# Mixer's last 32 tokens on a quarter of the array's columns, and a near 1/rms ahead of the exact one

## The chip, the cores and the metric

The kernel runs on one core of a Trainium2 chip. The metric is the device time of one execution in microseconds (us). TensorE (PE in the profile) multiplies, VectorE (DVE), ScalarE (ACT) and GpSimd (POOL) do the elementwise work, and SyncE (SP) issues the transfers. Each engine works its own queue in order; between engines there are semaphores.

## The reference, cut to what matters

The reference is a decoder trunk of two layers over 272 tokens (16 meta tokens and 256 others) of width 1024. Each layer is a half-step SwiGLU FFN, a mixer, and another half-step FFN, each between two RMSNorms. The first layer's mixer is a causal pooling mixer, the second layer's is differential attention. The part that the change is about is the pooling mixer and the norm behind it:

```python
def causal_multiscale_pool(h, w, b, scale):     # windows 2, 4, 8, 16 over four groups of 256 columns
    ...
    for g, win in enumerate(POOL_WINDOWS):
        lo = jnp.maximum(t + 1 - win, 0)
        cnt = (t + 1 - lo).astype(jnp.float32)
        pooled.append((csg[:, 1:, g] - csg[:, lo, g]) / cnt[None, :, None])
    diff = (jnp.stack(pooled, axis=2) - hg).astype(h.dtype)
    y = jnp.einsum('blgc,gcd->blgd', diff, w) + b
    return y.reshape(bsz, L, D) * scale
# in the trunk
    m = causal_multiscale_pool(rmsnorm(h, mix_norm_pre[i]), pool_w[j], pool_b[j], pool_scale[j])
    h = h + rmsnorm(m, mix_norm_post[i])
    f = swiglu(rmsnorm(h, ffn_norm_pre[i, 1]), ffn_w1[i, 1], ffn_w3[i, 1], ffn_w2[i, 1])
```

## The kernel before, in words

The residual h lies with the 1024 columns on partitions, as eight tiles of 128 x 272 (j = 0 to 7). The kernel has four FFN stages (ffn(0) to ffn(2) and last_ffn), the pooling mixer (`pool_mix`) between ffn(0) and ffn(1), and attention with its output projection (`attn_out`) between ffn(2) and last_ffn. Large products are made of three fp32r matmuls each: weights and activations are split into a high part (ACT, line 136: `whi`; `xhi`) and a low part (DVE, line 148: `wlo`; `xlo`), and lines 254 to 256 multiply high by high, high by low, low by high. Elsewhere matmuls are plain fp32, and the profile shows two records (two weight loads, two matmuls) for each of these.

The order of work on PE, ACT, DVE and SP is the order in which the program is written; no scheduler moves anything there.

**The mixer.** `inner(j)` (line 673) multiplies each h tile by its 128 x 256 weight `wp`, as soon as the tile has got the residual of ffn(0): line 691 makes the product `pt`, line 692 adds it to `h`, all on DVE in row pairs (1), (2, 3), (4, 5), (6, 7). Its output is token-major, for three blocks of tokens: 0 to 127, 128 to 255, and the last 128, of which only the last 32 matter (16 tokens and the 16 meta tokens, which stand last). ACT squares h (line 694, `psq`), DVE sums the squares (lines 698 to 701, `pacc`), and PE adds them over partitions (line 703, `sums`). From this comes 1/rms for each token (lines 280 and 274 to 276, `ny`), and ACT and DVE copy the inner products out of the PSUM banks scaled by it (lines 712 to 717, `zs`). `pooled(j)` (lines 725, 726, 729) then multiplies by constant band matrices (`bands`), which do the windowed mean and the subtraction.

**Behind the mixer.** ACT squares each y_j (line 445, `sq`), DVE sums the squares (line 456) and makes some of the scaled tiles `bt` (line 438: j = 0, 3, 4 in between, and j = 1, 2, 5 of `BESIDE` at the end). `post.rms` sums over partitions (lines 462 and 463), and line 280 makes 1/rms, `ny`. The first three tiles of ffn(1)'s input are made ahead from it: `rt` = b * ny (line 311), `xhi` = a + rt (line 313), where `a` (line 424) and `b` (line 429) were made earlier by ACT. `first_blocks` (line 514) then runs PE over these three (`go`), and goes on with the tiles that need the refined 1/rms (`refine`, lines 494, 326, 497, 328; then `tile`, lines 343 to 358), of which the first here is tile 3.

The three other such places already have a near 1/rms: the last squares are rounded to fp32r (line 470, `sqr`) and summed by single-pass matmuls (line 480), PE starts with the high parts, and the exact sum follows later (line 488).

**The output projection.** In `attn_out` ACT squares and scales each of the first five outputs (lines 445 and 436) between the splits of weights (line 136); `lows` (line 1043) waits for the squares of line 470.

Of the kernel before, what the change touches and what calls it, by code (L numbers as in the profile page):

```python
# [41 lines left out]
OUT_TABLE = 2  # L42

# [8 lines left out]
LATE = 2  # L52

POOL_H = ((0, 1), (1, 2), (2, 4), (4, 6), (6, 8))
POOL_SQ = ((0, 2), (2, 4), (4, 6), (6, 8))
# [10 lines left out]
BESIDE = (1, 2, 5)  # L66
REFILL = (0, 0, 0, 0, 0, 0, 0, 2)
# [111 lines left out]
def trunk(ctx, tc, ht, w13a, w13b, w2t, w2n, wqkva, wqkv, wo, wp, lamv, mask, band, gpost, out):  # L179
# [214 lines left out]
    class Post:  # L394


        def __init__(self, n, gains, next_gain, ahead):
            self.n, self.gains, self.next, self.ahead, self.acc = n, gains, next_gain, ahead, None
            self.r = None
            self.near, self.nears = False, []  # L400
            self.ab = []
            self.bt = [None] * NK
            self.sq = [None] * NK
# [64 lines left out]
        def near_square(self, j, y):  # L468
            sq = tmp.tile([P, L], F32R, tag="rsq", name="sqr", bufs=3)
            nc.scalar.activation(out=sq[:, :self.n], in_=y, func=AF.Square)  # L470
            self.nears.append((j, sq))

        def rms_near(self, bank, eps=False):
# [9 lines left out]
            w.refill(1, held=0)  # L483
# [19 lines left out]
    def first_blocks(res, us, spans, sums, refill, order):  # L503
# [153 lines left out]
    def pool_mix(old, ps, post):  # L657
# [17 lines left out]

        with tc.tile_pool(name="poolw", bufs=1, reuse_waits="tile") as pw:
            sq = pw.tile([P, NK, L], F32, name="psq")
            zs = [pw.tile([P, D], F32, name=f"zs{ti}", tag=f"zs{ti}") for ti in range(3)]
            ys = []

# [8 lines left out]
            for lo, hi in POOL_H[1:]:  # L689
                t = pw.tile([P, 3, L], F32, tag="pt", name="pt", bufs=2)[:, :hi - lo]  # L690
                nc.vector.tensor_tensor(t, btall[:, lo:hi], old.r.unsqueeze(1).to_broadcast([P, hi - lo, L]), ALU.mult)
                nc.vector.tensor_tensor(hall[:, lo:hi], hall[:, lo:hi], t, ALU.add)
# [5 lines left out]
            nc.vector.tensor_tensor(acc, sq[:, 0:2], sq[:, 2:4], ALU.add)  # L698
            nc.vector.tensor_tensor(acc, acc, sq[:, 4:6], ALU.add)
            nc.vector.tensor_tensor(acc, acc, sq[:, 6:8], ALU.add)  # L700
            nc.vector.tensor_tensor(acc[:, 0], acc[:, 0], acc[:, 1], ALU.add)
            for ti, (t0, t1) in enumerate(tok):
                nc.tensor.matmul(sums[:, ti:ti + 1], lhsT=acc[:, 0, t0:t1], rhs=ones[:, 0:1], start=True, stop=True)
# [6 lines left out]
            def normed(q):  # L710
                at = slice(q * 512, (q + 1) * 512)
                nc.scalar.mul(out=zs[0][:, at], in_=z[q][0], mul=r2[:, 0:1])
                nc.vector.tensor_scalar(zs[1][:, at], z[q][1], r2[:, 1:2], None, ALU.mult)
                if q:
                    nc.vector.tensor_scalar(zs[2][:, at], z[q][2], r2[:, 2:3], None, ALU.mult)
                else:
                    nc.scalar.mul(out=zs[2][:, at], in_=z[q][2], mul=r2[:, 2:3])

            def pooled(j):
# [5 lines left out]
                nc.tensor.matmul(y[:, P:SEQ], lhsT=zs[1][:, c], rhs=bands[:, g, 0:P], start=True, stop=True)  # L725
# [542 lines left out]
```

## Time and profile before

| what | before |
|---|---|
| median of 3 runs | 956.22 us (955.8 to 956.35) |
| the profiled execution, its own time | 956.16 us |
| its span, first to last instruction | 954.4 us |
| PE / DVE / ACT / POOL busy | 942.7 / 610.2 / 502.9 / 15.3 us |
| mean granted TensorE clock | 0.999 |

The span is the time between the first and the last instruction that the profiler recorded; the 1.76 us that the execution's own time has more lie around it. The busy times are unions of records. PE's records overlap and their ends are modelled, so a busy PE is not a PE at its best; where PE waits is read from the starts of its records and from the chain of waits.

### The profile page before, as it was taken

What the parts mean: (1) busy time and instruction counts of PE and PEld (TensorE: products, weight loads), DVE (VectorE), ACT (ScalarE), POOL (GpSimd) and SP (SyncE); (2) the same over time, 40 slices, a digit from 0 to 9 for tenths busy, and PEclk for the clock granted to TensorE, in tenths of its full rate; (3) what the DMA queues carried; (4) which work ended last, traced back from release to release, by engine and by line L of the source; (5) the groups of instructions that cost most, each with busy time, mean ns of one, the idle gap of its engine ahead of it and who ended that gap; (6) DMA issues with size and microseconds to landing.
All of it is one profiled execution on the core that took longest, in us unless ns stands there. A gap on an engine that the chain in (4) does not pass through costs nothing.

```text
span 954.4 us, 17970 instructions
## 1 busy us (share of the span) xinstructions
PE 942.7 (99%) x7241; PEld 918.6 (96%) x7241; DVE 610.2 (64%) x1054; ACT 502.9 (53%) x865; POOL 15.3 (2%) x22
## 2 busy tenths in 40 slices
PE   9999999999999999999999999999999999999997
PEld 9999999998999999999999999999998999999996
DVE  7955554458975555448855554478877898555553
ACT  7744444435654445545744455446767766444432
POOL 0000000210000000000000000000001000000000
PEclk9999999999999999999999999999999999999999
DMA  9765557630375556551755566522533628555521
GB/s 333 242 203 178 168 157 217 223 113 1 133 260 171 171 160 200 175 191 45 255 187 177 166 174 191 179 98 90 177 103 119 221 100 298 183 193 180 179 84 44
DMA packets 48322, 160.77 MB, mean 168 GB/s; under 512 B 5360, under 2 KB 8944, under 8 KB 48240
## 3 DMA queue, kind: packets, MB, share of 16 engines
q1 hardware_dynamic: 47952, 159.31, 51.3%
q8 instruction: 56, 0.92, 0.4%
q10 hardware_dynamic: 288, 0.33, 0.1%
q14 instruction: 26, 0.21, 0.1%
HBM read 158.57 MB, written 1.05 MB: 167 GB/s over the span
## 4 chain that ended last, share of the span: by engine, by line
PE 94%; DVE 3%; ACT 2%; issue 1%; DVEq 0%; POOL 0%; ACTq 0%; POOLq 0%
PE bank L256 26%; PE bank L255 26%; PE bank L254 26%; PE bank L514 8%; ACT whi L136 1%; PE bank L626 1%; PE bank L638 1%; PE bank L627 1%; PE bank L268 0%; ACT sc L827 0%; PE bank L804 0%; PE bank L795 0%; PE bank L794 0%; DVE h L343 0%; PE bank L1043 0%
## 5 line engine op out<-in xcount | busy, mean ns | idle before, releaser
L148 DVE TENSOR_TENSOR wlo<-raw,whi 128x1024 fp32r<-128x1024 f32 (+1 forms) x296 | 353.3, 1197 | 58.7 <-PE bank L255 28.5
L254 PE MATMUL bank<-xhi,whi 128*128 128x272 f32 (+1 forms) x1360 | 390.8, 287 | 0.0
L256 PE MATMUL bank<-xlo,whi 128*128 128x272 f32 (+1 forms) x1360 | 390.2, 287 | 0.0
L255 PE MATMUL bank<-xhi,wlo 128*128 128x272 f32 (+1 forms) x1360 | 389.0, 286 | 0.2 <-DVE wlo L148 0.2
L136 ACT CAST whi<-raw 128x1024 fp32r<-128x1024 f32 (+1 forms) x296 | 299.8, 1029 | 50.8 <-PE bank L256 45.9
L255 PEld LDWEIGHTS bank<-xhi,wlo 128*128 128x128 f32 x1360 | 256.0, 188 | 1.0 <-DVE wlo L148 0.4
L254 PEld LDWEIGHTS bank<-xhi,whi 128*128 128x128 f32 x1360 | 256.0, 188 | 1.0 <-issue 0.4
L256 PEld LDWEIGHTS bank<-xlo,whi 128*128 128x128 f32 x1360 | 256.5, 189 | 0.0
L255 PE MATMUL bank<-ghi,wlo 128*128 128x272 f32 x484 | 140.2, 290 | 0.0
L254 PE MATMUL bank<-ghi,whi 128*128 128x272 f32 x484 | 140.1, 289 | 0.0
L256 PE MATMUL bank<-glo,whi 128*128 128x272 f32 x484 | 140.0, 289 | 0.0
L556 ACT ACTIVATE ua<-ua 128x272 f32<-128x272 f32 (+1 forms) x88 | 37.0, 429 | 143.3 <-DVE ua L551 143.3
L562 DVE TENSOR_TENSOR ua<-bank,ua 128x272 f32<-128x272 f32 (+1 forms) x88 | 37.6, 435 | 93.6 <-PE bank L256 93.6
L565 ACT CAST ghi<-ua 128x272 fp32r<-128x272 f32 (+1 forms) x88 | 36.2, 418 | 110.6 <-DVE ua L562 110.6
L551 DVE TENSOR_TENSOR ua<-bank,ny 128x272 f32<-128x272 f32 (+1 forms) x88 | 37.6, 435 | 88.8 <-PE bank L256 88.8
L254 PEld LDWEIGHTS bank<-ghi,whi 128*128 128x128 f32 x484 | 91.9, 190 | 0.0
L256 PEld LDWEIGHTS bank<-glo,whi 128*128 128x128 f32 x484 | 91.4, 189 | 0.0
L255 PEld LDWEIGHTS bank<-ghi,wlo 128*128 128x128 f32 x484 | 91.0, 188 | 0.0
L456 DVE TENSOR_TENSOR pacc<-pacc,sq 128x272 f32<-128x272 f32 (+1 forms) x34 | 14.9, 438 | 42.0 <-ACT sq L445 41.5
L514 PE MATMUL bank<-xhi,whi 128*128 128x272 f32 (+1 forms) x240 | 38.0, 295 | 1.8 <-DVE xhi L313 1.7
L571 DVE TENSOR_TENSOR glo<-ua,ghi 128x272 fp32r<-128x272 f32 (+1 forms) x88 | 37.2, 431 | 0.5 <-ACT ghi L565 0.5
L514 PE MATMUL bank<-xhi,wlo 128*128 128x272 f32 (+1 forms) x240 | 36.9, 290 | 0.0
(207 smaller groups left out, 926.5 us busy)
## 6 DMA issues: line engine op xcount, KB each, us to landing
raw<-in_w13b SPq DMA_DIRECT2D x152, 512.0 KB, 3.8
raw<-in_w2t SPq DMA_DIRECT2D x48, 448.0 KB, 3.4
raw<-in_w2t SPq DMA_DIRECT2D x24, 512.0 KB, 3.6
raw<-in_w2n SPq DMA_DIRECT2D x22, 512.0 KB, 3.3
raw<-in_w13a SPq DMA_DIRECT2D x18, 512.0 KB, 3.3
raw<-in_wqkv SPq DMA_DIRECT2D x18, 512.0 KB, 3.4
raw<-in_wo SPq DMA_DIRECT2D x8, 512.0 KB, 3.2
raw<-in_wqkva SPq DMA_DIRECT2D x6, 512.0 KB, 3.2
```

Source lines behind the costliest of these rows:

```text
L136: self.nc.scalar.copy(out=hi[:, :n], in_=self.raws[u][:, :n])
L148: self.nc.vector.tensor_tensor(lo[:, :n], raw[:, :n], hi[:, :n].bitcast(F32), ALU.subtract)
L254: nc.tensor.matmul(out_ap, lhsT=a[0], rhs=b[0], start=start, stop=False)
L255: nc.tensor.matmul(out_ap, lhsT=a[1], rhs=b[0], start=False, stop=False)
L256: nc.tensor.matmul(out_ap, lhsT=a[0], rhs=b[1], start=False, stop=stop)
L456: nc.vector.tensor_tensor(acc[:, :n], self.acc[:, :n], sq[:, :n], ALU.add)
L514: nc.tensor.matmul(us[q][:, :n], lhsT=taken[u][a][:, c * P:(c + 1) * P], rhs=x[:, :n], start=start, stop=stop)
L551: nc.vector.tensor_tensor(a[:, :self.n], u1[:, :self.n], self.r2[:, :self.n], ALU.mult)
L556: nc.scalar.activation(out=a[:, :self.n], in_=a[:, :self.n], func=AF.Silu)
L562: nc.vector.tensor_tensor(s[:, :n], u3[:, :n], s[:, :n], ALU.mult)
L565: nc.scalar.copy(out=hi, in_=s[:, :n])
L571: nc.vector.tensor_tensor(lo, s[:, :self.n], hi.bitcast(F32), ALU.subtract)
```

## The change

Five things change.

1. The inner product of the last 32 tokens gets a bank of its own, `ze`, with one group of columns on each quarter of its partitions: eight matmuls with 32 stationary columns (`inner_ends`), behind `sums`. `inner` is left with two blocks of tokens. To give the sums for that bank, POOL adds the last 32 columns of the two halves of the squares, four times side by side (`spread`).
2. 1/rms is no longer applied to the inner products but to the band matrices: the products are copied out plainly, and ACT, DVE and POOL scale the bands (`sb`). `post.old` (`a`) is made behind this.
3. POOL adds the residual to h tiles 6 and 7 (`update`), the order of `inner` becomes 0, 1, 2, 3, 6, 7, 4, 5, and the squares and their sums follow it.
4. The mixer's last two squares (j = 6, 7) are rounded to fp32r for a near 1/rms (`rms_near`). The exact squares come later, and the exact sum and the refinement are done behind the second of the three tiles that were made ahead (`exact_at = 1`).
5. In `attn_out`, the scaled tiles 2 and 3 are made by DVE instead of ACT (`OUT_VECTOR`).

```diff
+OUT_VECTOR = (2, 3)
+POOL_NEAR = 6
...
@@ Post
-            if bias is None:
+            if bias is None and vector:
+                nc.vector.tensor_scalar(o, y, g, None, ALU.mult)
+            elif bias is None:
                 nc.scalar.mul(out=o, in_=y, mul=g)
@@ first_blocks
-            if k == EXACT[res.n] and res.post.near:
+            if res.post.near and k == res.post.exact_at:
                 res.post.exact()
                 res.refine()
@@ pool_mix
-        tok = ((0, P), (P, 2 * P), (L - P, L))
+        tok = ((0, P), (P, 2 * P))
+        ze = bank()
...
+        def inner_ends():
+            for j in (0, 2, 4, 6, 1, 3, 5, 7):
+                g = slice(j // 2 * 32, j // 2 * 32 + 32)
+                nc.tensor.matmul(ze[g, 0:256], lhsT=h[j][:, L - 32:L], rhs=wps[j], start=j % 2 == 0, stop=j % 2 == 1)
...
+            def update(engine, lo, hi):
+                t = pw.tile([P, 2, L], F32, tag="pt", name="pt", bufs=3)[:, :hi - lo]
+                engine.tensor_tensor(t, btall[:, lo:hi], old.r.unsqueeze(1).to_broadcast([P, hi - lo, L]), ALU.mult)
+                engine.tensor_tensor(hall[:, lo:hi], hall[:, lo:hi], t, ALU.add)
...
-            for lo, hi in POOL_H[1:]:
-                t = pw.tile([P, 3, L], F32, tag="pt", name="pt", bufs=2)[:, :hi - lo]
-                nc.vector.tensor_tensor(t, btall[:, lo:hi], old.r.unsqueeze(1).to_broadcast([P, hi - lo, L]), ALU.mult)
-                nc.vector.tensor_tensor(hall[:, lo:hi], hall[:, lo:hi], t, ALU.add)
-            for lo, hi in POOL_SQ:
-                nc.scalar.activation(out=sq[:, lo:hi], in_=hall[:, lo:hi], func=AF.Square)
-            for j in range(NK - LATE):
+            update(nc.gpsimd, 6, 8)
+            update(nc.vector, 1, 2)
+            inner(0)
+            inner(1)
+            squares(0, 2)
+            update(nc.vector, 2, 4)
+            inner(2)
+            inner(3)
+            squares(2, 4)
+            update(nc.vector, 4, 6)
+            squares(6, 8)
+            squares(4, 6)
+            for j in (6, 7, 4, 5):
                 inner(j)
+            nc.scalar.copy(out=zs[0][:, 0:512], in_=z[0][0])
+            nc.scalar.copy(out=zs[1][:, 0:512], in_=z[0][1])
...
+            nc.gpsimd.tensor_tensor(spread, two[0], two[1], ALU.add)
+            nc.vector.tensor_tensor(total, acc[:, 0], acc[:, 1], ALU.add)
             for ti, (t0, t1) in enumerate(tok):
-                nc.tensor.matmul(sums[:, ti:ti + 1], lhsT=acc[:, 0, t0:t1], rhs=ones[:, 0:1], start=True, stop=True)
-            for j in range(NK - LATE, NK):
-                inner(j)
+                nc.tensor.matmul(sums[:, ti:ti + 1], lhsT=total[:, t0:t1], rhs=ones[:, 0:1], start=True, stop=True)
+            nc.tensor.matmul(sums[:, 2:3], lhsT=spread.rearrange("p a b -> p (a b)"), rhs=ones[:, 0:1], start=True, stop=True)
+            inner_ends()
+            nc.vector.tensor_copy(zs[1][:, 512:1024], z[1][1])
+            nc.scalar.copy(out=zs[0][:, 512:1024], in_=z[1][0])
+            r2 = rsqrt(sums, 3, True, "rc", 3)
+            for q in range(2):
+                g = slice(2 * q, 2 * q + 2)
+                nc.scalar.mul(out=sb[:, g, 0:P + NMETA], in_=bands[:, g, 0:P + NMETA], mul=r2[:, 0:1])
+                nc.vector.tensor_scalar(sb[:, g, 176:], bands[:, g, 0:P], r2[:, 1:2], None, ALU.mult)
+                nc.gpsimd.tensor_scalar(sb[:, g, P + NMETA:176], bands[:, g, P + NMETA:], r2[:, 2:3], None, ALU.mult)
+                if q == 0:
+                    nc.scalar.copy(out=zse, in_=ze[:, 0:256])
             for j in range(post.ahead):
                 post.old(j)
-            r2 = rsqrt(sums, 3, True, "rc", 3)
...
-                post.squared(j, y[:, :L], vt[:, C_PS + j:C_PS + j + 1], pbs[:, j:j + 1], add=False)
-                if j:
+                if j >= POOL_NEAR:
+                    post.near_square(j, y[:, :L], vt[:, C_PS + j:C_PS + j + 1], pbs[:, j:j + 1])
+                else:
+                    squared(j)
+                if 0 < j <= POOL_NEAR:
                     post.add(j - 1)
...
-            for j in range(1, post.ahead):
-                first(j)
+            first(1)
             for j in BESIDE:
                 scaled(j, True)
-            post.rms(lambda: s, True)
+            post.rms_near(lambda: s, True, 0)
+            for j in range(POOL_NEAR, NK):
+                squared(j)
+            for j in range(2, post.ahead):
+                first(j)
             for j in range(NK):
                 if j not in EARLY + BESIDE:
                     scaled(j)
+            post.exact_at = 1
@@ attn_out
-            post.scaled(j, ys[j][:, :n])
+            post.scaled(j, ys[j][:, :n], vector=j in OUT_VECTOR)
```

In the rows below, a name is a tile, `x6` says how many instructions of the kind follow one another, and the shape is that of the result. PE between the residual of ffn(0) and the first `pooled`, before:

```order
L268 MATMUL bank<-ones 128x128 x12
L673 MATMUL bank<-wp,h 128x256 x18
L703 MATMUL bank<-ones,pacc_2635 128x1 x3
L673 MATMUL bank<-wp,h 128x256 x6
L725 MATMUL bank<-bands,zs_2590 128x128
L726 MATMUL bank<-bands,zs_2589 128x144
L729 MATMUL bank<-bands,zs_2591 128x2x16
```

and PE at the same place after the change:

```order
L267 MATMUL bank<-ones 128x128 x12
L674 MATMUL bank<-wp,h 128x256 x16
L731 MATMUL bank<-ones,ptotal 128x1 x2
L732 MATMUL bank<-ones,spread 128x1
L680 MATMUL bank<-wp,h 32x256 x8
L754 MATMUL bank<-sb,zs_2589 128x128
L755 MATMUL bank<-sb,zs_2588 128x144
L758 MATMUL bank<-sb,zse 128x2x16
```

All sixteen inner products now stand ahead of the sums, and the eight quarter products stand where six whole ones stood.

DVE from the residual's factor `r` to the sum of the squares, before:

```order
L501 SCALAR_TENSOR_TENSOR r_2599<-nt,ny 128x272
L691 TENSOR_TENSOR pt<-bt,r_2599 128x272
L692 TENSOR_TENSOR h<-h,pt 128x272
L691 TENSOR_TENSOR pt<-bt,r_2599 128x544
L692 TENSOR_TENSOR h<-h,pt 128x544
L691 TENSOR_TENSOR pt<-bt,r_2599 128x544
L692 TENSOR_TENSOR h<-h,pt 128x544
L691 TENSOR_TENSOR pt<-bt,r_2599 128x544
L692 TENSOR_TENSOR h<-h,pt 128x544
L698 TENSOR_TENSOR pacc_2635<-psq 128x544
```

and what POOL has in all after the weights `wp` of the mixer, after the change (before, the first and the last of these rows follow one another):

```order
L650 TENSOR_SCALAR wp<-wp,h 128x256 x8
L690 TENSOR_TENSOR pt<-bt,r_2598 128x544
L691 TENSOR_TENSOR h<-h,pt 128x544
L727 TENSOR_TENSOR spread<-pacc_2634 128x128
L742 TENSOR_SCALAR sb<-bands,ny 128x2x32 x2
L421 TENSOR_SCALAR a<-h 128x256 x4
```

The last pair of DVE's rows of `pt` and `h` (lines 691 and 692, 544 elements) has moved to POOL, where it stands beside the three pairs that DVE keeps.

PE at the start of ffn(1), before:

```order
L463 MATMUL bank<-sq,ones 128x272
L514 MATMUL bank<-xhi,whi 128x272 x6
L514 MATMUL bank<-xhi,wlo 128x272 x6
L514 MATMUL bank<-xhi,whi 128x272 x6
L514 MATMUL bank<-xhi,wlo 128x272 x6
L514 MATMUL bank<-xhi,whi 128x272 x6
L514 MATMUL bank<-xhi,wlo 128x272 x6
```

and after the change:

```order
L481 MATMUL bank<-sqr,ones_r 128x272 x2
L515 MATMUL bank<-xhi,whi 128x272 x6
L515 MATMUL bank<-xhi,wlo 128x272 x6
L515 MATMUL bank<-xhi,whi 128x272 x6
L515 MATMUL bank<-xhi,wlo 128x272 x6
L489 MATMUL bank<-pacc,ones 128x272
L515 MATMUL bank<-xhi,whi 128x272 x6
L515 MATMUL bank<-xhi,wlo 128x272 x6
```

The exact sum (line 489) stands between the second and the third of the tiles made ahead, and the third is all that PE has between the exact sum and tile 3.

More of the change, by code (lines that the diff above doesn't have):

```diff
@@ L466, in rms, with near_square, rms_near @@
             self.y = rsqrt_table(self.s, n, eps, "r1")
[L468 removed]
+        def near_square(self, j, y, scale=1.0, bias=0.0):
             sq = tmp.tile([P, L], F32R, tag="rsq", name="sqr", bufs=3)
[L470 removed]
+            nc.scalar.activation(out=sq[:, :self.n], in_=y, func=AF.Square, scale=scale, bias=bias)
             self.nears.append((j, sq))
[L473 removed]
+        def rms_near(self, bank, eps=False, refill=1):
             n = self.n
@@ L1242, in _layout @@
     count = np.minimum(np.concatenate([t[NMETA:], t[:NMETA]]) + 1, win)
+    each = np.where((d >= 0) & (d < win), 1.0 / count, 0.0) - (d == 0)
     ends = np.zeros((P, 4, 2 * NMETA))
-    ends[P - NMETA:] = np.where((d >= 0) & (d < win), 1.0 / count, 0.0) - (d == 0)
+    for g in range(4):
+        ends[g * 32 + NMETA:g * 32 + 32, g] = each[:, g]
     r["band"] = c(np.concatenate([inside, ends], axis=2).astype(np.float32))
```

39 lines of the change are left out of this document (17 added, 22 removed).

## The prediction

> **What bounds the kernel now.** I read the page first: how much of the span is PE, and what the chain of waits is made of.
>
> ```profile
> PE 942.7 (99%) x7241; PEld 918.6 (96%) x7241; DVE 610.2 (64%) x1054; ACT 502.9 (53%) x865; POOL 15.3 (2%) x22
> PE 94%; DVE 3%; ACT 2%; issue 1%; DVEq 0%; POOL 0%; ACTq 0%; POOLq 0%
> ```
>
> PE bounds nearly everything; the 6% of the chain on DVE and ACT lies where the stages meet. So the second view is the chain of waits between ffn(0) and ffn(1) (start, us, engine, line):
>
> ```profile
> 209.94 0.45 DVE pt L691
> 210.42 0.44 DVE h L692
> ...
> 213.65 0.65 DVE pt L691
> 214.32 0.74 DVE h L692
> ...
> 217.88 0.83 PE bank L703 x6
> 218.70 2.70 PE bank L673 x12
> ...
> 226.94 0.58 ACT sq L445
> 227.52 0.48 ACT b L429
> 228.02 1.50 DVE bt L438 x3
> 229.52 0.36 DVE rt L311
> ...
> 230.49 0.61 PE bank L514 x3
> ```
>
> DVE's residual and sums lead to line 703 at 217.88, two inner products on PE to `pooled`, PE's eight `pooled` to the last square, and then neither PE nor `ny` but ACT's `b` and three `bt` on DVE to the first `xhi`. From the end of the last square to ffn(1) it is 230.49 - 227.52 = 2.97 us. The third view is the order of time, for what stands beside this chain:
>
> ```profile
> 209.59 8.19 PE L673 MATMUL bank<-wp,h 128*128 128x256 f32 x36
> 212.33 5.05 PEld L673 LDWEIGHTS bank<-wp,h 128*128 128x128 f32 x24 [0.23 <-issue]
> 215.65 1.33 ACT L424 ACTIVATE a<-h 128x272 f32<-128x272 f32 x3
> 219.50 0.16 DVE L276 SCALAR_TENSOR_TENSOR ny<-nt,ny 128x3 f32<-128x3 f32 x1
> 221.24 0.39 PE L725 MATMUL bank<-bands,zs 128*128 128x128 f32 x2
> 222.05 0.58 ACT L445 ACTIVATE sq<-bank,pbs,h 128x272 f32<-128x272 f32 x1 [0.51 <-PE bank L729]
> 222.53 0.57 ACT L429 ACTIVATE b<-bank,pfirst 128x272 f32<-128x272 f32 x1
> 222.99 1.72 ACT L445 ACTIVATE sq<-bank,pbs,h 128x272 f32<-128x272 f32 x3
> ```
>
> PE's 36 records (18 inner products) end at 217.78, just ahead of the sums: PE and DVE arrive there together.
>
> **The change part by part.**
>
> *Inner products to the sums.* Six tiles were multiplied between 209.59 and 217.78, and the last four of them, 24 records, from 212.33 on without a pause: 0.227 us a record. The new order has 32 records there: tile 0, tile 1 (when h is there, at 210.9) and, from 212.33, tiles 2, 3, 6, 7, 4, 5 with 24 records. These end at 212.33 + 24 x 0.227 = 217.78 again. DVE, with two instructions of 0.65 and 0.74 less, would be ready 1.4 us sooner, and gains nothing, since PE is late next. Worth: 0, if tiles 6 and 7 are there when PE has done tile 3, at 212.33 + 8 x 0.227 = 214.15.
>
> *Tiles 6 and 7 on POOL.* This is the unknown: no row has POOL at two instructions of 544 elements, or POOL reading two tiles. The nearest rows are its scalings of 256 elements, alone and beside an instruction of DVE that reads two tiles:
>
> ```profile
> 166.93 1.83 POOL L649 TENSOR_SCALAR wp<-wp,h 128x256 f32<-128x256 f32 x1 [165.28 <-PE bank L255]
> 166.94 1.10 DVE L148 TENSOR_TENSOR wlo<-raw,whi 128x896 fp32r<-128x896 f32 x1 [1.09 <-issue]
> 174.95 0.93 POOL L649 TENSOR_SCALAR wp<-wp,h 128x256 f32<-128x256 f32 x1 [5.29 <-DMA wp<-in_wp]
> 175.27 1.10 DVE L148 TENSOR_TENSOR wlo<-raw,whi 128x896 fp32r<-128x896 f32 x1 [1.02 <-issue]
> 175.85 1.31 POOL L649 TENSOR_SCALAR wp<-wp,h 128x256 f32<-128x256 f32 x1
> ```
>
> Alone it is 0.93 us. Where a `wlo` of DVE is running, POOL ends 0.72 (168.76 behind 168.04) or 0.79 us (177.16 behind 176.37) behind that instruction's end, whenever it began: it waited for DVE. A price for 544 elements and two inputs lies between 0.72 (DVE's own) and 0.93 x 544/256 x 2 = 3.9 us; I take 0.79 x 544/256 = 1.7, near the rows' own engine. Now DVE does nothing but two-input instructions from 209.94 to 213.65 (the end of `h` for tiles 4 and 5), with 0.03 us between them. Two things can happen. Either POOL comes in only behind them: tiles 6 and 7 are ready at 213.65 + 2 x 1.7 = 217.05, PE's last four tiles take 16 x 0.227 = 3.63, and the sums start at 220.7 instead of 217.78: 2.9 later (0.95 at the low price). Or POOL comes in between, and DVE waits for it in turn: POOL 210.39 to 212.09, `h` of tile 1 to 212.53, then POOL's second instruction to 214.23 and tiles 2 and 3 to 215.63, from where PE has 24 records to do: 221.1, 3.3 later; 1.65 later if POOL's second instruction comes in only behind tiles 2 and 3, and 1.4 at the low price. I take 2.6 as the middle of these, with 0 (no hindrance) to 3.4 as ends.
>
> The Trainium skill, page "SBUF — State Buffer", section "Who interferes with whom", says that DVE instructions with two SBUF inputs and GpSimd instructions that read SBUF share one read interface, taken for a whole instruction, so that the other fully blocks. The rows agree as far as POOL's waiting goes (1.83 beside DVE, 0.93 alone); that DVE waits for POOL no row shows, as the DVE instruction at 175.27, 0.32 us into POOL's, kept its 1.10. By that rule the second of the two ways is left, at +1.65 to +3.3; without it the first is as likely, and the sum is the same within 0.5.
>
> *From the sums to `pooled`.* 1/rms is ready at 219.66 as before (the copies of the products end beside the sums). Then `pooled` waits for the scaled bands instead of the last two inner products: ACT has 288 elements to scale, like an `a` (0.41 from start to start, 1.33 for three), so PE starts at about 220.2 instead of 221.24. The quarter products must be done by then:
>
> ```profile
> 657.33 0.45 PE bank L794 x4
> 657.79 0.46 PE bank L795 x4
> 431.18 1.52 PE bank L514 x12
> 432.71 0.46 PE bank L488 x2
> ```
>
> Attention's scores are fp32 on halves of the rows: two products of 144 and two of 272, which one after the other would take 2 x 0.24 + 2 x 0.46 = 1.4 (0.46 for 272 from the last row) and take 0.91: the halves run side by side. No row has quarters of the columns; between 0.9 (four at once) and 16 x 0.227 = 3.6 us (one by one) I take the former, and they end at 219.5, hidden under the reciprocal root. POOL's small scaling of the bands may come 0.3 late. The three `a` of ACT, hidden before, now delay its squares: 0.41 (bands) + 0.35 (`zse`) + 0.41 + 1.33 behind 219.66 gives 222.15 for the first square, 1.1 behind PE. ACT then does a square in 0.46 where it does not wait (222.53 to 222.99) and PE a `pooled` in 0.69, so ACT has caught up at the sixth: the last square ends at about 226.5 instead of 227.52. Behind it stand, as before, `b`, three `bt` and `rt`, 2.97 us; the near sum replaces 0.62 of fp32 matmul by single passes, but `ny` is not what is waited for. Worth: -1.0 (-0.7 to -1.05).
>
> *The exact sum behind the second tile.* Where a near root is used already, the order of time shows what follows the exact sum:
>
> ```profile
> 433.20 0.49 ACT L280 ACTIVATE ny<-bank,zero_c 128x272 f32<-128x272 f32 x1 [1.20 <-PE bank L488]
> 435.62 0.52 ACT L349 ACTIVATE xhi<-h 128x272 fp32r<-128x272 f32 x1 [1.46 <-DVE h L343]
> 233.69 0.52 ACT L349 ACTIVATE xhi<-h 128x272 fp32r<-128x272 f32 x1 [3.10 <-DVE h L343]
> ```
>
> From the exact sum's start (432.71) to the refined `xhi` (435.62 + 0.52) it is 3.43, and 0.1 until PE has it: 3.53. There, two more tiles ahead cover it. Here PE has the sum itself (0.46) and one tile of 12 matmuls, 1.5 (the row of 431.18): it then stands still for 3.53 - 1.97 = 1.57. Before, tile 3's `xhi` was there at 234.21 and PE needed it only at 230.49 + 3 x 1.5 = 235.0. Cost: 0.46 + 1.57 = +2.0 (1.7 to 2.2). DVE's later tiles keep their lead over PE: they shift by more, but were 1.5 us ahead.
>
> *The output projection.* Two scalings of 0.36 leave ACT, and PE's wait of 0.40 for `sqr` goes:
>
> ```profile
> 754.66 1.21 PE L1043 MATMUL bank<-olo,whi 128*128 128x256 f32 x8 [0.40 <-ACT sqr L470]
> 753.58 3.49 DVE L148 TENSOR_TENSOR wlo<-raw,whi 128x1024 fp32r<-128x1024 f32 x3
> 757.19 0.43 DVE L311 TENSOR_TENSOR rt<-b,ny 128x256 f32<-128x256 f32 x1
> ```
>
> DVE is late next: it gets the two scalings, its three `wlo` still end at about 757.1, and `rt` starts behind them, not behind `ny`. Worth: -0.1 (-0.5 to +0.2).
>
> **Sum**, against the profiled execution's own 956.16 (span 954.4; 0.06 under the median): 0 + 2.6 - 1.0 + 2.0 - 0.1 = +3.5, so 959.7. 0.2% is 1.9 us, about what a measurement of this kernel can tell from no change.
>
> **The rivals.**
>
> *POOL is not hindered, and the kernel is not slower.* If POOL's two instructions take under 2.1 us each and run beside DVE's, tiles 6 and 7 are there by 214.15 and the first term is 0: +0.9, 957.1, inside 0.2%. It decides at 1.0 us of delay, tiles ready at 215.1. For it: the price of 1.7 would do. Against it: in the rows with both engines POOL waits each time.
>
> *The quarters run one by one*, so that the change does not do what it says: they end at 222.2, `zse` at 222.6, and the first `pooled` at 222.7 instead of 222.0, so that the -1.0 becomes +0.7. With POOL hindered 961.4, without 958.8. Against it: the halves of the scores.
>
> *The wait behind the exact sum is covered.* If PE did not stand still at all, 2.0 would be 0.46: with POOL free 955.6, hindered 958.2. Against it: the 3.53 is a chain of dependent steps, each waiting for the last, and its length is measured.
>
> **How the numbers follow.** POOL hindered with the rest as summed: 0.55 (958.3 to 960.6). Quarters one by one: 0.05. POOL free: 0.29. Wait covered with POOL free: 0.06. Faster by over 1.9 us asks for the last and 1.5 us more that no row offers: 0.05. So slower 0.60, within 0.2% 0.35, faster 0.05. The time is the likeliest case's. The range goes from 956.6 (POOL free, a little better) to 961.0, and leaves out 1 in 10 on either side.
>
> **What would show it.** In the profile after: POOL's two instructions at lines 690 and 691 over 1.5 us each or DVE's beside them stretched, and PE waiting at line 674 for `h`; the sums (line 731) near 220.4 instead of 217.88; the eight products of line 680 within 1 us; from the sums to the first `xhi` matmul 11.6 instead of 12.6; and at line 515, behind line 489, a wait of PE of 1.6 us for `xhi`. I am wrong if POOL ends before 214.2, or if PE has no gap behind line 489.

## The result, and the profile after

| | before | after |
|---|---|---|
| median | 956.14 us (6 executions, 955.8 to 958.6) | 961.45 us (6 executions, 959.47 to 963.98) |
| after / before | | 1.0053 [1.0043, 1.0062] |
| the profiled execution | 956.16 us, span 954.4, clock 0.999 | 962.48 us, span 960.7, clock 0.995 |

The changed kernel is 0.53% slower. The forecast was 959.7 us with a range up to 961.0: the direction was right, and the time lies 0.45 us above the range. The six executions differ from one another by 4.5 us, and they go with the granted clock: 959.47 us at 0.998, 961.07 at 0.997, 961.35 and 961.56 at 0.996, 962.48 at 0.995, 963.98 at 0.992.

The page of the changed kernel, first the busy time of each engine and then the chain's share by engine, hardly differs from the page of before:

```profile
PE 943.5 (98%) x7243; PEld 918.5 (96%) x7243; DVE 611.6 (64%) x1055; ACT 504.4 (53%) x869; POOL 18.9 (2%) x27
PE 93%; DVE 3%; ACT 2%; issue 1%; DMA 0%; POOL 0%; DVEq 0%; POOLq 0%; ACTq 0%
```

The place is found in the chain of waits between ffn(0) and ffn(1) (start, us, engine, line; `x24` is a run of 24 records):

```profile
209.66 1.57 POOL pt L690
211.29 1.43 POOL h L691
...
214.15 6.90 PE bank L674 x24
221.05 0.34 PE bank L731 x4
...
232.58 4.85 PE bank L515 x24
237.43 0.64 PE bank L489 x2
```

Before, this chain ran over DVE's `pt` and `h`; now it runs over POOL's. From the first DVE `pt` (209.94 before, 209.59 after) to the sums over the partitions it was 217.88 - 209.94 = 7.94 us and is 221.05 - 209.59 = 11.46: +3.52. From the sums to the first `xhi` matmul of ffn(1) it was 230.49 - 217.88 = 12.61 and is 232.58 - 221.05 = 11.53: -1.08. From there to the first matmul that needs the refined 1/rms it was 4.59 and is 241.08 - 232.58 = 8.50: +3.91 (both rows stand further down). The sum is +6.35; the two profiled executions differ by 962.48 - 956.16 = 6.32. So the loss lies in this stretch: what stands ahead of it is 0.35 us shorter (209.94 - 209.59), what stands behind it some 0.3 longer, and the two cancel.

The end of the third stretch before is read in the order of time of the kernel before. Its three tiles ahead are six groups of six matmuls from 230.49 on; here are the second group and the first one of tile 3, and 235.08 - 230.49 is the 4.59:

```profile
231.31 0.91 PE L514 MATMUL bank<-xhi,wlo 128*128 128x272 f32 x6
...
235.08 0.92 PE L514 MATMUL bank<-xhi,whi 128*128 128x272 f32 x6
```

**Where POOL and DVE meet.** DVE's rows in order of time, after, and then POOL's:

```profile
209.59 0.44 DVE L690 TENSOR_TENSOR pt<-bt,r 128x272 f32<-128x272 f32 x1
210.06 1.45 DVE L691 TENSOR_TENSOR h<-h,pt 128x272 f32<-128x272 f32 x1
211.44 1.85 DVE L690 TENSOR_TENSOR pt<-bt,r 128x544 f32<-128x544 f32 x1
213.32 0.72 DVE L691 TENSOR_TENSOR h<-h,pt 128x544 f32<-128x544 f32 x1
```

```profile
209.66 1.56 POOL L690 TENSOR_TENSOR pt<-bt,r 128x544 f32<-128x544 f32 x1 [15.74 <-DVE r L502]
211.29 1.41 POOL L691 TENSOR_TENSOR h<-h,pt 128x544 f32<-128x544 f32 x1
```

DVE's `h` of tile 1 takes 1.45 us instead of 0.44, and its next `pt` 1.85 instead of some 0.72, the price of the next row's instruction of the same shape. Each of the two ends behind an instruction of POOL: 211.51 behind POOL's end at 211.22, 213.29 behind 212.70. And POOL's first instruction, issued while DVE's first `pt` ran, ends 1.19 us behind the end of that `pt` (210.03); its second ends 212.70 - 211.51 = 1.19 behind the end of DVE's `h`. Both engines wait in turn: first POOL for DVE, then DVE for POOL, twice.

PE's rows at the same place (idle time before, and what ended it, in the brackets):

```profile
209.23 1.10 PE L674 MATMUL bank<-wp,h 128*128 128x256 f32 x4
211.62 1.10 PE L674 MATMUL bank<-wp,h 128*128 128x256 f32 x4 [1.28 <-POOL pt L690]
214.15 6.90 PE L674 MATMUL bank<-wp,h 128*128 128x256 f32 x24 [1.44 <-issue]
...
221.55 1.07 PE L680 MATMUL bank<-wp,h 128*32 128x256 f32 x16
```

PE stands still for 1.28 us ahead of tile 1 and for 1.44 ahead of tile 2: DVE's `h` of tile 1 ends at 211.51, that of tiles 2 and 3 at 214.04, and PE starts 0.11 behind each, whatever the brackets name. Then its 24 records take 6.90 us; the forecast had 24 x 0.227 = 5.45. The eight quarter products, 16 records, take 1.07 us together.

**What the granted clock did.** The table by stretches (bounds, length, busy time of PE, PEld, DVE, ACT, POOL with their instructions, then the granted clock, DMA share and GB/s) shows what the other views hide:

```profile
212.00:215.00 3.00, 1.56 (x6) 1.08 (x5) 2.93 (x4) 1.12 (x3) 0.71 (x1) 0.79 0.00 0
215.00:218.00 3.00, 3.00 (x10) 2.44 (x10) 2.69 (x5) 1.86 (x4) 0.12 (x1) 0.64 0.01 3
233.00:236.00 3.00, 3.00 (x18) 2.81 (x17) 1.72 (x5) 0.83 (x2) 0.00 (x0) 0.70 0.02 5
236.00:239.00 3.00, 3.00 (x18) 2.86 (x17) 0.39 (x1) 0.87 (x2) 0.00 (x0) 0.73 0.00 0
```

Inside these the clock is 0.50 in a part and 1.00 in the rest, as narrower stretches show:

```profile
214.10:217.00 2.90, 2.85 (x7) 2.34 (x8) 2.67 (x4) 1.85 (x3) 0.00 (x0) 0.50 0.00 0
234.50:237.20 2.70, 2.70 (x13) 2.70 (x13) 0.29 (x1) 0.00 (x0) 0.00 (x0) 0.50 0.00 0
```

So the time at half clock is (1 - 0.79) x 3 / 0.5 = 1.26 plus (1 - 0.64) x 3 / 0.5 = 2.16, together 3.42 us; at the second place 1.80 + 1.62 = 3.42 us again. It ends 2.16 behind 215.00, at 217.16, and began at 213.74; the second lasts from 234.20 to 237.62. Between the two beginnings lie 20.46 us, six times 3.41. PE's work that falls into the first (from 214.15 on) loses half of 3.01 us, 1.5; into the second, half of 3.42, 1.7. In the kernel before the clock of this place is 1.00:

```profile
227.00:233.00 6.00, 4.30 (x30) 3.63 (x29) 5.30 (x14) 3.20 (x7) 0.00 (x0) 1.00 0.01 3
```

The Trainium skill, page "TensorE: Matmul & The Clock Gate", Part 1, has a window of 3413 ns that runs freely and a clock of either half or full; the length, the grid and the two values agree with this trace. It has the half clock follow an idle window. Here PE was not idle in the 3.41 us ahead of the second half-clock window: it began `xhi` matmuls at 232.58, 1.62 us ahead of 234.20. The measurement decides: here a window in which PE stood still for about half the time, 1.62 of 3.41 us, was enough.

**The start of ffn(1).** PE's rows after, in order of time, with one of its weight loads:

```profile
232.58 1.22 PE L515 MATMUL bank<-xhi,whi 128*128 128x272 f32 x6 [1.62 <-DVE xhi L312]
233.41 0.19 PEld L515 LDWEIGHTS bank<-xhi,whi 128*128 128x128 f32 x1 [0.18 <-ACT bt L441]
233.64 1.07 PE L515 MATMUL bank<-xhi,wlo 128*128 128x272 f32 x6
...
241.08 1.02 PE L515 MATMUL bank<-xhi,whi 128*128 128x272 f32 x6 [1.52 <-ACT xhi L348]
```

PE waits 1.52 us behind the exact sum. There is also a small wait that is new: the sixth matmul of the first tile needs a bank that ACT frees with `bt` (line 441). ACT now has the two exact squares ahead of that, and the first six matmuls take 233.64 - 232.58 = 1.06 us from start to start instead of 231.31 - 230.49 = 0.82.

### The profile page after: what moved, and what is told of

Its sections match the earlier page's. It is cut to its first block, busy times and chain, and to the rows that moved or that the text cites. A ratio compares the mean times of both kernels' runs of the same rounds, so it can differ in the third digit from the quotient of the medians.

```text
span 960.7 us, 17976 instructions
## 1 busy us (share of the span) xinstructions
PE 943.5 (98%) x7243; PEld 918.5 (96%) x7243; DVE 611.6 (64%) x1055; ACT 504.4 (53%) x869; POOL 18.9 (2%) x27
## 3 DMA queue, kind: packets, MB, share of 16 engines
HBM read 158.57 MB, written 1.05 MB: 166 GB/s over the span
## 4 chain that ended last, share of the span: by engine, by line
PE 93%; DVE 3%; ACT 2%; issue 1%; DMA 0%; POOL 0%; DVEq 0%; POOLq 0%; ACTq 0%
PE bank L255 26%; PE bank L254 26%; PE bank L253 26%; PE bank L515 8%; PE bank L674 1%; DVE wlo L147 1%; PE bank L627 1%; PE bank L639 1%; PE bank L628 1%; DMA raw<-in_w13a 0%; ACT sc L864 0%; DVE h L342 0%; PE bank L841 0%; PE bank L832 0%; PE bank L831 0%
## 5 line engine op out<-in xcount | busy, mean ns | idle before, releaser
L253 PEld LDWEIGHTS bank<-xhi,whi 128*128 128x128 f32 x1360 | 255.8, 188 | 1.0 <-issue 0.4
L515 PEld LDWEIGHTS bank<-xhi,whi 128*128 128x128 f32 x240 | 33.4, 193 | 5.7 <-ACT xhi L348 2.0
```

The source lines that it names most:

```text
L253: nc.tensor.matmul(out_ap, lhsT=a[0], rhs=b[0], start=start, stop=False)
L515: nc.tensor.matmul(us[q][:, :n], lhsT=taken[u][a][:, c * P:(c + 1) * P], rhs=x[:, :n], start=start, stop=stop)
```

## The experiments

Ratios are against the kernel before, on the same chip (one chip for the x and z runs, another for the y runs).

| kernel | what it is | median us (executions) | ratio |
|---|---|---|---|
| x1_fill | after, PE's four pauses filled | 959.40 (5) | 1.0034 [1.0021, 1.0047] |
| x2_dve | after, tiles 6 and 7 on DVE | 958.74 (10) | 1.0023 [1.0014, 1.0033] |
| x3_rms | after, near 1/rms undone | 959.21 (10) | 1.0025 [1.0016, 1.0034] |
| x4_dve_rms | both undone | 956.96 (10) | 1.0010 [1.0001, 1.0019] |
| y1_x4_fill | x4 with one pause filled | 956.36 (10) | 1.0003 [0.9993, 1.0012] |
| y2_before_fill | before with the same pause filled | 956.00 (10) | 0.9999 [0.9989, 1.0009] |
| y3_pool_reads | x4, one more POOL instruction that reads | 957.85 (1) | |
| y4_pool_writes | x4, one more POOL instruction that only writes | 958.17 (1) | |
| z1_ahead4 | x2 with four tiles ahead | 957.75 (11) | 1.0016 [1.0007, 1.0025] |
| z2_before_ov | before with `OUT_VECTOR` | 956.10 (11) | 0.9997 [0.9988, 1.0006] |

### x1_fill: is the half clock the missing part?

Products of a constant tile that nobody reads stand in PE's four pauses, so that PE is busy while it would wait. Everything else is the changed kernel.

```diff
             inner(0)
+            warm(lambda: idle, ones, 5, P)
             inner(1)
+            warm(lambda: idle, ones, 5, P)
...
+            if i == 1:
+                res.fill = lambda: warm(lambda: s2, ones, 6, P)     # behind the third tile ahead
+                warm(lambda: us[0], ones, 6, P)                     # ahead of the first
             first_blocks(res, us, [n] * 6,
```

> The changed kernel with dummy fp32 matmuls in PE's four pauses: five behind the inner products of tile 0, five behind those of tile 1, six ahead of the first tile made ahead, six behind the third (0.24 us each, so each batch is shorter than or as long as its pause). Theory 1 (POOL and DVE hold each other up, PE stands still, and the TensorE clock falls because it stood still): the waits stay, the clock does not fall; 24 records of inner products in 5.5 us instead of 6.9, granted clock 0.999, time 959.2 +- 0.6, and the runs lie within 1 us of each other instead of 4.5. Rival (the clock falls for another reason, such as what is multiplied there): clock 0.996 and 961.4 as without the dummies.

Measured: 959.40 us (959.17 to 960.11), at clocks of 0.998 to 0.999. The table by stretches of the profiled execution has the full clock at both places:

```profile
212.00:218.00 6.00, 5.68 (x31) 5.00 (x32) 5.71 (x7) 3.27 (x6) 0.95 (x1) 1.00 0.01 4
233.00:239.00 6.00, 5.81 (x46) 5.55 (x45) 3.54 (x10) 1.76 (x4) 0.00 (x0) 1.00 0.00 0
```

and PE's rows have the 24 records at the forecast's pace again, with the idle products (line 267) in between:

```profile
209.46 1.10 PE L680 MATMUL bank<-wp,h 128*128 128x256 f32 x4
210.40 1.28 PE L267 MATMUL bank<-ones 128*128 128x128 f32 x10
...
214.39 5.42 PE L680 MATMUL bank<-wp,h 128*128 128x256 f32 x24 [0.32 <-issue]
...
231.25 1.32 PE L516 MATMUL bank<-xhi,whi 128*128 128x272 f32 x6 [0.19 <-DVE xhi L313]
...
238.32 1.02 PE L516 MATMUL bank<-xhi,whi 128*128 128x272 f32 x6 [0.19 <-ACT xhi L349]
```

The idle products take nothing away from the waits: tile 2 starts 214.39 - 209.46 = 4.93 us behind tile 0, as in the changed kernel (214.15 - 209.23 = 4.92). Only the clock changed, and with it 2 us of the median and most of the spread (0.9 us instead of 4.5). What is left, +3.3 us, is what the change costs at full clock; the forecast had said +3.5. The three pieces can be read here without the half clock. The first DVE `pt` is at 209.82 and the sums' piece of the chain at 219.81, so 9.99 us (+2.05 against the kernel before); then 231.25 - 219.81 = 11.44 (-1.17), and 238.32 - 231.25 = 7.07 (+2.48). Together that is +3.36.

### x2_dve, x3_rms, x4_dve_rms: which part costs what

x2 gives tiles 6 and 7 to DVE, in the order of the new `inner`:

```diff
-            update(nc.gpsimd, 6, 8)
...
+            update(nc.vector, 6, 8)
             update(nc.vector, 4, 6)
```

> The changed kernel with the residual of tiles 6 and 7 added by DVE, between tiles 2, 3 and tiles 4, 5. Theory 1: DVE's h of tile 1 is back at 0.44 us and the next pt at 0.72; PE does not wait for tile 2; the sums start 8.3 us behind the first inner product (11.7 in the changed kernel); the wait of 1.5 us behind the exact sum stays. Time 957.0 if the clock holds behind it, up to 958.7 if it falls there. Rival (the new order of tiles and squares delays PE, not POOL): the sums still start 11 us behind and the time is over 960.

x3 keeps POOL and takes the near 1/rms back:

```diff
-                if j >= POOL_NEAR:
-                    post.near_square(j, y[:, :L], vt[:, C_PS + j:C_PS + j + 1], pbs[:, j:j + 1])
-                else:
-                    squared(j)
+                squared(j)
...
-            post.rms_near(lambda: s, True, 0)
+            post.rms(lambda: s, True)
...
-            post.exact_at = 1
```

> The changed kernel without the near 1/rms of the mixer: all eight squares exact, the sum once, no refinement behind the second tile. Theory 1: PE's 0.46 and its wait of 1.5 us go, and what the clock loses there (up to 1.7), while the three bt on DVE keep the start of the first tile where it is: 958.2 to 959.9, that is 2 to 3.5 under the changed kernel. Rival (the near root brings forward what the exact sum costs): the first tile starts about 1 us later and the time stays at 961.

x4 has both edits, so that the quarter products, the scaled bands and `OUT_VECTOR` are what is left of the change.

> Both undone: DVE adds all residuals, no near 1/rms; left of the change are the quarter products, the scaled bands and the order of tiles. Theory 1: the -1.0 of the prediction alone, 955.1 +- 0.4, clock 0.999. Rival (the quarter products or the scaled bands cost something themselves): 956.1 or more.

x2: 958.74 us. PE's rows of its profiled execution show no wait at the inner products worth the name:

```profile
211.74 5.42 PE L674 MATMUL bank<-wp,h 128*128 128x256 f32 x24 [0.29 <-issue]
217.32 0.60 PE L731 MATMUL bank<-ones,ptotal 128*128 128x1 f32 x4 [0.17 <-DVE ptotal L729]
```

With its first DVE `pt` at 209.32, the sums come 8.00 us later, against 7.94 before: POOL was all of the first loss. The rest of its chain of waits:

```profile
229.12 4.92 PE bank L515 x24
...
237.62 12.33 PE bank L515 x96
```

From the sums to the first `xhi` matmul it is 11.80, a gain of 0.81; from there to the refined tile 8.50, as in the changed kernel, with one half-clock window. At 0.998 its executions are at 957.86 to 958.46, at 0.996 and 0.997 at 959.01 to 959.59. Expected were 957.0 with the clock held and 958.7 without: the executions lie 0.3 to 1.5 us above these, of which 0.4 is placed under z1.

x3: 959.21 us, in two groups: four executions at clock 0.999, 957.33 to 958.18, and six at 0.997, 959.13 to 959.90. Its profiled execution is of the first group, with the same two pauses as the changed kernel, and without a half-clock window:

```profile
211.47 1.10 PE L674 MATMUL bank<-wp,h 128*128 128x256 f32 x4 [1.28 <-POOL pt L690]
214.00 5.42 PE L674 MATMUL bank<-wp,h 128*128 128x256 f32 x24 [1.43 <-issue]
```

So the pauses don't always bring the half clock. The other group's 0.997 and its 1.8 us are the size of one half-clock window, though no execution of it was profiled. That fits a free-running window: whether one window gets enough of the idle time depends on where it begins. Where it begins in an execution that was not profiled can't be seen; that it is the position that decides remains argued. At full clock POOL costs 9.98 - 7.94 = 2.04 us here (first `pt` at 209.44, the sums' piece of the chain at 219.42), the first `xhi` matmul comes 12.28 behind the sums (-0.33), and PE then runs 132 records without a pause. That makes +1.7; measured +1.3 to +2.1 for the four executions at 0.999. The median is within the expected range, but the first tile did not stay where it was: it starts 12.28 behind the sums, 0.75 later than in the changed kernel. In this point the rival was nearer.

x4: 956.96 us; five executions at 0.999 between 955.98 and 956.56, five at 0.994 to 0.997 between 957.35 and 959.11. This missed: without POOL and without the exact sum I had expected the gain of 1 us behind the sums to be left over, and there is none, even in the executions at full clock. The chain of waits from the last squares on shows why:

```profile
226.20 0.45 DVE pacc L457
...
226.75 0.45 DVE pacc L457
...
227.25 0.73 PE bank L463 x2
...
228.47 0.50 ACT ny L279
...
230.05 2.15 PE bank L515 x8
```

The chain now runs over DVE's sums of the squares, the exact sum on PE and `ny`; before, it ran over ACT's last square, `b` and `bt`. The sums stand at 217.51 and the first `xhi` matmul at 230.05, 12.54 later, against 12.61 before. The near sum, which takes the last two squares past DVE's `pacc`, is thus what lets the earlier squares count: quarter products and scaled bands gain 0.07 without it (0.33 in x3), 0.81 with it (1.08 in the changed kernel). The near sum in turn brings the wait behind the exact sum, which costs more.

### y1_x4_fill and y2_before_fill: the clock without the change

By the mean clock, five of x4's ten executions hold a stretch at half clock. In the profiled one it lies between the last square and ffn(1):

```profile
227.00:233.00 6.00, 4.13 (x17) 3.65 (x18) 5.53 (x14) 2.47 (x6) 0.00 (x0) 0.73 0.01 3
```

y1 puts six idle products into PE's pause ahead of ffn(1), and y2 does the same to the kernel before:

```diff
+            if i == 1:
+                warm(lambda: us[0], ones, 6, P)
             first_blocks(res, us, [n] * 6,
```

> DVE adds all residuals and there is no near 1/rms, as in the run before, and PE gets six dummy matmuls in its pause ahead of ffn(1)'s first tile. In the run before, a window of 3.4 us at half clock lay behind that pause in about half of the executions (957.3 to 959.1 with it, 956.0 to 956.6 without). Theory 1 (the clock falls where PE stands still): all executions at 0.999 and 955.9 to 956.5, spread under 0.7 us. Rival (the window has another cause): executions over 957 remain.

> The kernel before with the same six dummies in the same pause (1.69 us). Theory 1: PE is busy enough ahead of it, with the third block of tokens, that the clock falls in few executions only: median within 0.2 us of before (956.1), and its rare executions over 957 go. Rival (the dummies gain something by themselves): 0.5 us or more faster.

y1: 956.36 us, nine of ten executions between 955.76 and 956.59, one at 957.77 (clock 0.998). No execution over 957 was expected, and no profile shows what made this one late. The same stretch of its profiled execution, at full clock:

```profile
227.00:233.00 6.00, 5.01 (x35) 4.66 (x36) 5.46 (x14) 3.03 (x7) 0.00 (x0) 1.00 0.01 3
```

y2: 956.00 us, ten executions between 955.71 and 956.32. The kernel before, run beside it, has three of 19 at 957.11 to 957.77 with a clock of 0.997; with the pause filled there is none in ten. So filling a pause gains nothing by itself. That it takes the late executions away is shown for the changed kernel, by x1; these two runs point the same way, but none in ten against three in 19 would come by chance about one time in four. And what is left of the change in x4 is within the uncertainty of no change.

### y3_pool_reads and y4_pool_writes: what holds DVE

Both are x4 with one instruction more on POOL beside DVE's `pt` and `h` of tile 1, with a result that nobody needs. In y3 it reads 544 elements and scales them; in y4 it only writes 544 elements (a one-element copy of DVE ahead of it sets the moment).

```diff
+            dm = pw.tile([P, 2, L], F32, name="dm")
+            nc.gpsimd.tensor_scalar(dm, btall[:, 6:8], old.r[:, 0:1], None, ALU.mult)    # y3
+            nc.vector.tensor_copy(dm[:, 0, 0:1], old.r[:, 0:1])                          # y4
+            nc.gpsimd.memset(dm, 0.0)                                                    # y4
             update(nc.vector, 1, 2)
```

> As the run with both undone, but POOL scales tiles 6 and 7 of bt (544 elements, one input) into a tile that nobody uses, as soon as r is there, beside DVE's residuals; it is extra work. Theory 1 (a POOL instruction that reads SBUF and a DVE instruction with two SBUF inputs exclude each other): POOL ends about 0.8 to 1.1 us behind DVE's first pt, and DVE's h of tile 1 takes 0.8 to 1.2 us instead of 0.44. Rival (only POOL's two-input instructions hold DVE up): h takes 0.44.

> The same with POOL filling that tile with zeros, so that it only writes; one tiny DVE copy ahead of it makes it start at the same time. Theory 1: no DVE instruction there is longer than its usual 0.44 or 0.72 us, and POOL does not wait either. Rival (it is any POOL instruction that holds DVE up): DVE's pt or h of tile 1 is stretched as with the reading one.

In order of time, y3, DVE and POOL:

```profile
210.37 0.84 DVE L691 TENSOR_TENSOR h<-h,pt 128x272 f32<-128x272 f32 x1
...
209.98 1.86 POOL L705 TENSOR_SCALAR dm<-bt,r 128x544 f32<-128x544 f32 x1 [16.11 <-DVE r L502]
```

and y4:

```profile
210.11 0.44 DVE L691 TENSOR_TENSOR h<-h,pt 128x272 f32<-128x272 f32 x1
...
209.85 0.55 POOL L706 MEMSET dm<- 128x544 f32 x1 [16.29 <-DVE dm L705]
```

Beside a POOL instruction that reads one input, DVE's `h` of tile 1 takes 0.84 instead of 0.44; beside one that only writes, 0.44 as alone. So it is reading that holds the other engine, and the row of the forecast in which DVE was not held (the `wlo` at 175.27) did not stand for this case; why DVE kept its 1.10 us there stays open (the same happened at 183.59, 1.09 us beside a POOL instruction from 183.18 on). Each of the two is one execution. POOL's scaling ended later than expected, 211.84 - 210.33 = 1.51 us behind DVE's first `pt` instead of 0.8 to 1.1. The Trainium skill, page "SBUF — State Buffer", section "Who interferes with whom", says this of a DVE instruction with two inputs against a GpSimd instruction that reads, and exempts one that only writes: both halves agree with y3 and y4, and the two `wlo` rows of the kernel before do not fit. The same page, section "SBUF: two separate sides", says that the hold lasts for the whole instruction. For two-input instructions the rows nearly agree (DVE's `h` of tile 1 ends 0.29 behind POOL's end, where it takes 0.44 alone); for the one-input scaling they don't: DVE's `h` ends at 211.21, though POOL's instruction lasts to 211.84 by its record (the profile's records of POOL are rough).

### z1_ahead4: can the wait behind the exact sum be covered?

x2 with a fourth tile ahead, so that two tiles of work stand behind the exact sum, and with the idle products against the half clock ahead of the first tile:

```diff
-AHEAD = (0, 3, 4, 4, 4)
-ORDER = (O1, O3, OA, OA, OA)
+AHEAD = (0, 4, 4, 4, 4)
+ORDER = (O1, OA, OA, OA, OA)
...
+            if i == 1:
+                warm(lambda: us[0], ones, 6, P)
```

> The changed kernel with the residual's tiles 6 and 7 done by VectorE (between its calls for 2,3 and 4,5), with four tiles instead of three of the last blocks ahead, two of them now ahead of the exact sum's products... the tile that is added stands so that the products of three tiles run behind the exact sum, and with six idle matmuls ahead of the first tile against the half clock. Theory (the wait of 1.5 us behind the exact sum is a lack of cover): xhi arrives 3.5 us after the exact sum's products, the added cover makes it hidden but for the exact sum's own 0.5 us: the gain of 0.74 us ahead of it stays, so 956.1 - 0.7 + 0.5 = 955.9, 955.6 to 956.4. Rival (the near root's first tile can't be made up for, the wait only moves to the next tile or to a bank that comes free late): 957.4 or more, with a wait of PE over 1 us between the exact sum and the fifth tile.

Measured: 957.75 us (957.32 to 958.27, clocks 0.997 to 0.999). The time is the rival's, the wait is the theory's. PE's rows and two of its weight loads, in order of time:

```profile
230.30 1.79 PE L516 MATMUL bank<-xhi,whi 128*128 128x272 f32 x6 [0.20 <-DVE xhi L313]
231.23 0.19 PEld L516 LDWEIGHTS bank<-xhi,whi 128*128 128x128 f32 x1 [0.28 <-ACT b L429]
231.70 0.19 PEld L516 LDWEIGHTS bank<-xhi,whi 128*128 128x128 f32 x1 [0.28 <-ACT bt L442]
231.93 0.91 PE L516 MATMUL bank<-xhi,wlo 128*128 128x272 f32 x6
...
237.84 1.03 PE L516 MATMUL bank<-xhi,whi 128*128 128x272 f32 x6
```

The wait of 1.5 us behind the exact sum is gone. But a fourth tile ahead needs a fourth `a` and a fourth `b` from ACT. The `a` delays the squares: from the sums (218.19 in the chain) to the first `xhi` matmul it is 12.11 instead of x2's 11.80. The `b` delays the last banks: the first six matmuls take 231.93 - 230.30 = 1.63 instead of 0.82 before. From the first `xhi` matmul to the fifth tile it is 7.54 where the kernel before has 4.59 and one tile of 1.50, 6.09. So by the chain +0.06 (sums) - 0.50 + 1.45 = +1.0 against before; measured +1.6. Of the other 0.6, 0.4 lies outside the span: z1's executions are 2.18 us longer than their spans in the median, those of the kernel before 1.78. x2, x4 and y1 have 2.15 to 2.18 as well, the changed kernel, x1 and x3 1.77 to 1.81. No run shows why, but it is no part of the stretch that was changed. The last 0.2 is not placed. The cover is to be had, but ACT has no time for it there.

### z2_before_ov: the output projection alone

```diff
+OUT_VECTOR = (2, 3)
...
-            post.scaled(j, ys[j][:, :n])
+            post.scaled(j, ys[j][:, :n], vector=j in OUT_VECTOR)
```

> The kernel before with one edit: the attention's outer product of the last stage has its bands 2,3 put on VectorE as the changed kernel has it (OUT_VECTOR). The prediction priced this at -0.1 us: expected within 0.2 us of before, 955.7 to 956.3. Rival (the edit is worth half a microsecond or more, hidden in the other runs): 955.5 or less.

956.10 us, 0.9997 [0.9988, 1.0006]: no change that can be measured, as forecast. The interval alone reaches to -1.1 us and so doesn't exclude the rival's half microsecond; the medians, 0.07 us apart, and the shortest executions (955.47 and 955.55) speak against it.

## Why the prediction was right or wrong

The forecast's terms, against the changed kernel with the half clock taken off (1.45 in the first stretch, 6.90 - 5.45; 1.71 in the third), and against the experiments; x1 has them at full clock in one trace:

| term | forecast | after, without the half clock | by experiments |
|---|---|---|---|
| inner products to the sums, order and quarter products | 0 | | +0.06 (x2) |
| tiles 6 and 7 on POOL | +2.6 (0 to 3.4) | 3.52 - 1.45 = +2.07 | +2.05 (x1), +2.04 (x3) |
| sums to the first `xhi` | -1.0 (-0.7 to -1.05) | -1.08 | -1.17 (x1), -0.81 (x2); without the near sum -0.07 (x4), -0.33 (x3) |
| exact sum behind the second tile | +2.0 (1.7 to 2.2) | 3.91 - 1.71 = +2.20 | +2.48 (x1) |
| output projection | -0.1 (-0.5 to +0.2) | | -0.1 (-1.1 to +0.6, z2) |
| sum | +3.5 | +3.2 | +3.36 by x1's rows, +3.3 by its median |
| half clock | not in the sum | +3.0 to +3.2 here; by an estimate from the times 0 to some 4.5 over the executions | |

*POOL.* The mechanism was right, and it was the second of the two ways: POOL comes in between, and DVE waits for it in turn. POOL's instructions were cheaper than taken: each ended 1.19 us behind the end of the DVE instruction that it waited for, where the forecast counted 1.7, and so the term is 2.05 and not 2.6. PE waited at line 674, as said. The rival of a POOL that runs unhindered is out.

*The quarter products* run side by side, 1.07 us for 16 records, as taken from the scores; that rival is out.

*Sums to the first `xhi`.* 11.53 us, forecast 11.6. But the reason given was only half of it. The forecast said that `ny` is not what is waited for, and priced the near sum at nothing here. x4 shows that with the squares earlier the exact sum and `ny` are what ends last, so the near sum is a condition of the gain.

*The exact sum.* The wait is 1.52 us, forecast 1.57. The term is larger by 0.2 (after) to 0.5 (x1). Half of that or more is the bank that ACT frees late, for which the forecast had no row: the first six matmuls take 1.06 in the changed kernel and 232.41 - 231.25 = 1.16 in x1 instead of 0.82. The rival in which this wait is covered is out for the kernel as it is; z1 covers it and pays elsewhere.

*The step that failed* is one that the prediction used wherever it counted PE's work, and never weighed: that a record of PE takes the same time after a pause as before it ("24 x 0.227 = 5.45", "one tile of 12 matmuls, 1.5"). It counted PE's waits as time lost once. In the profiled execution they are lost a second time: behind both stretches of waits PE runs at half clock for 3.42 us, its 24 records take 6.90 instead of 5.45, and this, some 3 us, is not in the sum. That the half clock follows from the standing still is shown by filling the pauses; how much of a window it takes is read from two places only, where PE stood still for 2.31 us (1.28 + 1.03) and 1.62 us of the 3.41 ahead. The sum without the clock, 956.2 + 3.2, is 959.4, and the execution that shows 0.998 has 959.47. x1 fills the pauses, leaves the waits as they are, and comes to 959.40. That this is so near the forecast's 959.7 is in part luck: POOL was priced 0.55 too high and the exact sum 0.2 to 0.5 too low. The profile of before could not have shown it, as its clock at this place was 1.00; but it had a pause of 1.69 us in the same place, and among the executions measured later some, 957.1 to 957.8 at 0.997, were late.

## What to carry to other kernels

Where PE is the bound, a new wait of PE can cost twice: its own length, and the work behind it at half clock, here up to 1.7 us for each window; so look at the granted clock by stretches before calling a spread noise, and fill a pause that can't be avoided with products that nobody needs. Work given to POOL was not free where DVE did two-input work beside it: the two took turns, and the loss, 2.05 us, was of the size of POOL's two instructions, 1.19 each. A near sum in front of an exact one pays only if enough finished work stands between the exact sum and its first reader, and the engine that has to make that cover must have the time for it.

## What the runs showed of the hardware

- The granted clock falls to exactly 0.50 for 3.42 us at a time. In the changed kernel it did so where PE was idle 1.28 + 1.44 us, and where it was idle 1.62 us; pauses of the same length had the full clock in other executions (x3's 1.28 + 1.43, the 1.69 of the kernel before). Idle products of a constant tile in the pauses kept it at 1.00 in x1's profile.
- POOL's product or sum of two 128 x 544 inputs took 1.56 and 1.41 us, part of it waiting for DVE (1.19 behind DVE's end); the scaling of one such input 1.86 us with its wait; the writing of 544 elements 0.55 us.
- Eight fp32 products of 32 stationary columns by 256, two on each quarter of the columns, take 1.07 us in all; the same 16 records one by one would take 16 x 0.227 = 3.6, an estimate from the whole inner products.
